# Transposes of dilated queries and keys spread through the running projection block, the keys' bank taken from another PSUM pool

## The chip, the cores and the metric

The kernel runs on one core of a Trainium2 chip. The metric is device time in microseconds for one launch: 1484.63 is the median of three runs of the kernel before (1481.72 to 1486.92).

## The reference

Two layers of a decoder trunk with 512 positions and a width of 1024, in float32. Each layer normalises its input, makes one wide projection from it, and feeds three mixers: a gated convolution (A), a causal latent attention with 8 heads (B), and a dilated sliding-window attention with three groups of 8 heads (C). The part that the change touches is C:

```python
dq = rmsnorm(dq.reshape(B, S, DIL_GROUPS, DIL_HEADS, DIL_HEAD_DIM), dil_q_norm_g[:, None, :])
dk = rmsnorm(dk.reshape(B, S, DIL_GROUPS, DIL_HEADS, DIL_HEAD_DIM), dil_k_norm_g[:, None, :])
for gi, (window, dilation) in enumerate(DIL_PATTERNS):
    o_g, lse_g = dilated_group_attention(dq[:, :, gi], dk[:, :, gi], dv[:, :, gi], slopes[gi],
                                         dilation, window // dilation)
alpha = jax.nn.softmax(jnp.stack(lses, axis=0), axis=0)
o_c = jnp.sum(alpha[..., None] * jnp.stack(outs, axis=0), axis=0)
```

The branches are gated, projected back, merged, projected once more and added to the input.

## The kernel before

Every large product is made of three matmuls in a reduced float32 format: operands are split into a high and a low part, and high x high, high x low and low x high are added up in one PSUM bank (`mm3`, lines 118 to 122). For weights the split runs on the chip: ScalarE casts the high part (line 114), VectorE subtracts it (line 115). Weight buffers rotate by five (`W_RAW`, `W_BUF`).

TensorE's order is written out by hand (`manual_schedule`, line 56): it runs its instructions in the order in which the program emits them. The order of VectorE, ScalarE and the DMA queue on SyncE is found by a scheduler that goes by priorities. Each engine works through its own list strictly in order.

The bulk of TensorE's work is a *filler*, a generator (lines 938 to 960) that yields after every *step*; a step is mostly one `mm3` of 512 columns, that is three matmuls (lines 120, 121, 122). The attention code asks the filler for some steps between its own pieces, so that attention and projections interleave. In the filler stand, one after the other: three convolution tiles, four gate tiles of B, nine *dilated blocks* (`dil_block`, each 32 steps in four PSUM banks of 8 steps, with 512 of the 4608 columns of queries, keys and values of C), a fourth convolution tile, four gate tiles of C, and the merge.

C is worked through in 12 *units* per layer: unit u belongs to the pair of heads p = u // 3 and to the group g = u % 3. Once a unit's queries and keys are projected and normalised, they are transposed (`dil_t`, lines 637 to 667): four 128x128 transposes (line 646) of the queries into one PSUM bank, four of the keys into another. The bank is then emptied. For g = 1 and 2 that is one ScalarE instruction (line 665). For g = 0 each half of the partitions is scaled by ScalarE (line 656), then a remainder is taken by VectorE (line 660); for keys ScalarE writes a second copy as well (line 658). The transposes of a block's units stand in the next block, after its first 15 steps (`T_LAG`); before, all banks of these units follow each other there, as one step each. Units 0, 3, 4, 7, 8 and 11 stand alone in their block, units 1 and 2, 5 and 6, 9 and 10 share one. After the last bank of a pair's third unit `ready` lets that pair's attention begin.

PSUM has eight banks, handed out by pools: `tr` two, `sc` two, `pj` two, `pv` one, `p1` one. `tr` is used by all transposes: those of dilated queries and keys, those of the probabilities of B (`mla_trans`, line 492) and of C (`dil_trans`, lines 779 and 788, emptied by VectorE in line 781 and ScalarE in line 790). `p1` is used by the preparation of B (`mla_p1`, and line 452 for its keys), which is over before the first dilated transposes, and once at the start of a layer (line 224).

The attention of a pair (`dil_main`) first makes its scores in four *rounds* (`dil_scores`): matmuls into the two `sc` banks (lines 691 and 695 for g = 0, in two rounds; line 701 for g = 1 and g = 2), then VectorE empties them with the bias added (line 709) and ScalarE takes the exponential (line 712). Six filler steps stand between rounds (`DIL_A`), and a round needs both `sc` banks empty again.

Of the kernel before, what the change touches and what calls it, by code (L numbers as in the profile page):

```python
# [27 lines left out]

F_LORA, F_P1, F_P2, F_MLA, F_TAIL, N_TAIL = 24, 6, 10, 1.2, 5.0, 28
NV_POOL, N_WAKE = 1, 11  # L30
LAG, PV_LAG, T_LAG = 2, 2, 15
P1_AT, P2_AT = (0, 8, 16), (6, 14, 22)
L_STEPS = ((5, 7, 8), (2, 4, 8))
DIL_A, DIL_GAP, DIL_B, DIL_C = 6, 29, 2, 2
# [11 lines left out]
def hybrid_kernel(ctx: ExitStack, tc: tile.TileContext, a: dict):  # L46
# [13 lines left out]
    def nm(s):  # L60
        uid[0] += 1
        return f"{s}_{uid[0]}"

    def psum(tag):
        return pp.tile([P, 512], F32, tag=tag, name=nm(tag), bufs=1 if tag in ("pv", "p1") else 2)
# [4 lines left out]
    def t2(shape, dt=F32):  # L70
        return sp.tile(shape, dt, tag="c2", name=nm("c2"), bufs=C2)
# [90 lines left out]
    def tok_nat(c):  # L162
        return slice(c * P, (c + 1) * P)

    def to_chunks(t, r):

        return t.rearrange("p (c x) -> p x c", c=NCH)[:, 32 * r:32 * r + 32]
# [43 lines left out]
    ps = psum("tr")  # L211
# [6 lines left out]
    for l in range(DEPTH):  # L218
# [347 lines left out]
        def dil_block(b):  # L566

            u0 = b // 3 * 4
            pieces = [(u0 + i // 3, i % 3) for i in range(b % 3 * 4, b % 3 * 4 + 4)]
            for u, s in pieces:  # L570
                m, p, g = dil_unit(u)
                if s == 2:
                    m["v"][g] = t2([P, NCH, P])
                    if g == 0:
                        m["bias"] = sp.tile([P, 2, S], F32, tag="bias", name=nm("bias"), bufs=1)
                        after_weights(nc.sync.dma_start(m["bias"], a["bias"][2 * p:2 * p + 2].rearrange("h p n -> p h n")))

            runs = []
            for i, (u, s) in enumerate(pieces):
                if runs and runs[-1][1] == u:  # L580
                    runs[-1][3] += 1
                else:
                    runs.append([i, u, s, 1])
            wq = []
            for q in range(4):
                dmas = []
                for i, u, s, n in runs:
                    c0 = u % 3 * 512 + u // 3 * P
                    if n == 1:
                        dmas.append((0, 1024, lambda t, i=i: t.rearrange("p (k n) -> p k n", k=2)[:, :, i * P:i * P + P],  # L590
                                     w_dil[:, 2 * q:2 * q + 2, s, c0:c0 + P]))
                        continue
                    for k in range(2):
                        o = k * 512 + i * P
                        dmas.append((o, o + n * P, lambda t, n=n: t.rearrange("p (s n) -> p s n", s=n),
                                     w_dil[:, 2 * q + k, s:s + n, c0:c0 + P]))
                wq.append(split_weights(1024, dmas))

            def evac(c, ps):
                for i, u, s, n in runs:  # L600
                    m, p, g = dil_unit(u)
                    nqk = min(n, 2 - s) if s < 2 else 0
                    if nqk:
                        nc.scalar.copy(m["nat"][g][:, c, s * P:(s + nqk) * P], ps[:, i * P:(i + nqk) * P])
                    if nqk < n:
                        nc.scalar.copy(m["v"][g][:, c], ps[:, (i + nqk) * P:(i + n) * P])

            yield from proj_n(wq, 512, evac)
            for u, s in pieces:
                if s == 2 and u % 3 == 0:  # L610

                    vt = dil[u // 3]["v"][0]
                    vscr = dp.tile([S, P], F32, tag="vscr", name=nm("vscr"))
                    nc.sync.dma_start(vscr.rearrange("(r p) d -> p r d", p=P), vt)
                    nc.sync.dma_start(vt, vscr.rearrange("(p c) d -> p c d", p=P))
                if s == 1:
                    dil_norm(u)
# [19 lines left out]
        def dil_t(p, g):  # L637
            m = dil[p]
            nat = m["nat"][g]
            m["qkt"].append([])  # L640
            for i in range(2):
                ps = psum("tr")
                for c in range(NCH):

                    dst = to_chunks(ps, c) if g == 0 else ps[:, tok_nat(c)]
                    nc.tensor.transpose(dst, nat[:, c, i * P:(i + 1) * P], ident)  # L646
                gg = prm2[:, 24 + g:25 + g] if i == 0 else prm[:, O_DK + g:O_DK + g + 1]
                if g == 0:

                    st = [t2([P, S], F32R) for _ in range(2)]  # L650
                    if i == 1:
                        lo = t2([P, S], F32R)
                    for h in range(2):
                        own = slice(64 * h, 64 * h + 64)
                        oth = slice(64 - 64 * h, 128 - 64 * h)
                        nc.scalar.activation(st[h][own], ps[own], AF.Copy, scale=gg[own])
                        if i == 1:
                            nc.scalar.activation(st[h][oth], ps[own], AF.Copy, scale=gg[own])
                        dst = lo[own] if i else st[h][oth]
                        nc.vector.scalar_tensor_tensor(out=dst, in0=ps[own], scalar=gg[own], in1=st[h][own],  # L660
                                                       op0=ALU.mult, op1=ALU.subtract)
                    m["qkt"][g] += [st, lo] if i else [st]
                else:
                    qt = t2([P, S])
                    nc.scalar.activation(qt, ps, AF.Copy, scale=gg)
                    m["qkt"][g].append(qt)
                yield
# [261 lines left out]
                    merged.append(hl)  # L929


        def transposes(units):
            for u in units:
                yield from dil_t(u // 3, u % 3)
                if u % 3 == 2:
                    ready[0] = u // 3

        def filler():
            for f in range(3):
                yield from conv_tile(f)  # L940
            for f in range(4):
                yield from z_tile(C_BZ, ob, "b", f)
            prev = []
            for b in range(9):
                gen = dil_block(b)
                for i in range(T_LAG if prev else 0):
                    next(gen)
                    yield
                yield from transposes(prev)
                yield from gen  # L950
                prev = [b // 3 * 4 + i for i in ((0,), (1, 2), (3,))[b % 3]]
            gen = conv_tile(3)
            for _ in range(T_LAG):
                next(gen)
                yield
            yield from transposes(prev)
            yield from gen
            for f in range(4):
                yield from z_tile(C_CZ, oc, "c", f)
            yield from gates()  # L960
# [32 lines left out]
        for dt in range(KD):  # L993
# [4 lines left out]
            ps = psum("pj")  # L998
# [99 lines left out]
```

## Time and profile before

| | |
|---|---|
| Median of three runs | 1484.63 us (1481.72 to 1486.92) |
| Profiled execution | 1483.1 us, span 1481.3 us |
| Mean granted clock of TensorE | 0.991 |
| TensorE (PE) matmul busy | 1434.1 us, 97% |
| VectorE (DVE) busy | 867.0 us, 59% |
| ScalarE (ACT) busy | 698.6 us, 47% |
| GpSimd (POOL) busy | 118.4 us, 8% |
| DMA queue 1, share of 16 engines | 32.8% |
| Chain that ended last | PE 81%, DVE 11%, ACT 5% |

TensorE has work nearly all the time, so time is won or lost where it waits; its waits are listed by the instruction that waited and the one that released it. A row of the timeline gives the start, the duration, the engine, the line, the output tile, the input tiles, the shapes and how many instructions were merged; in brackets stand the idle time before it and what ended it. `PEclk` in a table of windows is the granted clock as a share of its full speed of 2.4 GHz.

### The profile page before, as it was taken

How to read it: one execution, taken by the hardware profiler on the slowest of the kernel's cores; microseconds unless marked ns; L12 is line 12 of the kernel's file. 1: busy time of each engine (PE TensorE's matmuls, PEld its weight loads, DVE VectorE, ACT ScalarE, POOL GpSimd, SP SyncE). 2: the span in 40 equal slices, each digit the busy share in tenths (PEclk: the TensorE clock that was granted, in tenths of full speed). 3: DMA queues.
4: the chain of work that ended last, by engine and by line, in shares of the span. 5: the costliest groups of instructions: out<-in, count | busy, mean ns of one | idle time of the engine just before them, and what ended most of it. 6: DMA issues, size and time to landing. Idle time of an engine off the chain costs nothing.

```text
span 1481.3 us, 20395 instructions
## 1 busy us (share of the span) xinstructions
PE 1434.1 (97%) x7262; PEld 1181.6 (80%) x7262; DVE 867.0 (59%) x2295; ACT 698.6 (47%) x1600; POOL 118.4 (8%) x149
## 2 busy tenths in 40 slices
PE   9899999999979999999999999999999899999998
PEld 8778878877767878888898788788787677888887
DVE  8587775665566744343576867655664756534341
ACT  7455565656463432332354565656464553322220
POOL 0021221010010000000000212110100100000000
PEclk9999999999989999999999999999999999999999
DMA  8232222423223323333532321243252323333322
GB/s 248 75 100 58 61 72 58 128 74 87 78 73 106 89 79 92 100 115 97 171 113 73 99 67 37 73 119 81 58 134 82 81 63 88 86 99 100 114 71 85
DMA packets 237813, 136.52 MB, mean 92 GB/s; under 512 B 19856, under 2 KB 229392, under 8 KB 237712
## 3 DMA queue, kind: packets, MB, share of 16 engines
q1 hardware_dynamic: 237712, 135.23, 32.8%
q8 instruction: 57, 0.93, 0.3%
q14 instruction: 44, 0.36, 0.1%
HBM read 128.58 MB, written 6.62 MB: 91 GB/s over the span
## 4 chain that ended last, share of the span: by engine, by line
PE 81%; DVE 11%; ACT 5%; issue 2%; DMA 1%; SPq 0%; DVEq 0%; ACTq 0%
PE pj L120 20%; PE pj L121 19%; PE pj L122 19%; PE sc L122 4%; PE sc L121 3%; PE sc L120 3%; DVE wlo L115 2%; PE pv L810 2%; PE tr L646 1%; DMA wraw<-w_in 1%; ACT whi L114 1%; PE sc L701 1%; PE pv L509 1%; DVE c L175 1%; DVE s16a L628 1%
## 5 line engine op out<-in xcount | busy, mean ns | idle before, releaser
L115 DVE TENSOR_TENSOR wlo<-wraw,whi 128x1024 fp32r<-128x1024 f32 (+3 forms) x225 | 271.9, 1210 | 228.5 <-ACT whi L114 220.0
L114 ACT CAST whi<-wraw 128x1024 fp32r<-128x1024 f32 (+3 forms) x225 | 231.5, 1029 | 346.9 <-PE pj L121 189.0
L120 PE MATMUL pj<-hhi,whi 128*128 128x512 f32 x760 | 307.0, 404 | 2.9 <-ACT c L863 1.6
L121 PE MATMUL pj<-hlo,whi 128*128 128x512 f32 x760 | 298.6, 393 | 0.3 <-DVE hlo L284 0.3
L122 PE MATMUL pj<-hhi,wlo 128*128 128x512 f32 x760 | 298.6, 393 | 0.0
L120 PE MATMUL pj<-whi,hhi 128*128 128x512 f32 x576 | 238.8, 415 | 0.0
L121 PE MATMUL pj<-wlo,hhi 128*128 128x512 f32 x576 | 226.5, 393 | 0.0
L122 PE MATMUL pj<-whi,hlo 128*128 128x512 f32 x576 | 226.5, 393 | 0.0
L120 PEld LDWEIGHTS pj<-hhi,whi 128*128 128x128 f32 x760 | 143.8, 189 | 31.7 <-issue 2.1
L122 PEld LDWEIGHTS pj<-hhi,wlo 128*128 128x128 f32 x760 | 143.6, 189 | 30.9
L121 PEld LDWEIGHTS pj<-hlo,whi 128*128 128x128 f32 x760 | 144.0, 189 | 25.4 <-DVE hlo L284 0.9
L122 PEld LDWEIGHTS pj<-whi,hlo 128*128 128x128 f32 x576 | 108.8, 189 | 24.1
L120 PEld LDWEIGHTS pj<-whi,hhi 128*128 128x128 f32 x576 | 109.5, 190 | 22.7 <-issue 2.3
L121 PEld LDWEIGHTS pj<-wlo,hhi 128*128 128x128 f32 x576 | 109.4, 190 | 17.1
L712 ACT ACTIVATE c<-c,e 128x128 f32<-128x128 f32 (+1 forms) x192 | 80.1, 419 | 36.1 <-DVE e L709 36.0
L634 POOL TENSOR_TENSOR c<-c,s16c 128x512 f32<-128x512 f32 x48 | 51.0, 1084 | 371.7 <-DVE s16c L103 199.2
L709 DVE CUSTOM_DVE_ANT_0 c<-sc,bias 128x128 f32<-128x128 f32 (+1 forms) x192 | 53.0, 319 | 41.4 <-PE sc L695 41.3
L120 PE MATMUL sc<-c,whi 128*128 128x512 f32 x192 | 75.4, 393 | 0.0
L122 PE MATMUL sc<-c,wlo 128*128 128x512 f32 x192 | 74.8, 389 | 0.0
L121 PE MATMUL sc<-c,whi 128*128 128x512 f32 x192 | 74.7, 389 | 0.0
L479 ACT ACTIVATE c<-c,mst 128x128 f32<-128x128 f32 (+1 forms) x64 | 36.0, 562 | 68.0 <-DVE mst L477 67.7
L917 DVE SCALAR_TENSOR_TENSOR c<-c,sc 128x512 f32<-128x512 f32 x48 | 33.0, 687 | 37.2 <-PE sc L122 37.2
(202 smaller groups left out, 2149.9 us busy)
## 6 DMA issues: line engine op xcount, KB each, us to landing
wraw<-w_in SPq DMA_DIRECT2D x96, 512.0 KB, 3.7
wraw<-w_in SPq DMA_DIRECT2D x96, 192.0 KB, 3.4
wraw<-w_in SPq DMA_DIRECT2D x144, 128.0 KB, 2.7
wraw<-w_o SPq DMA_DIRECT2D x16, 512.0 KB, 3.9
bias<-bias SPq DMA_DIRECT2D x8, 512.0 KB, 3.8
wraw<-w_out_a SPq DMA_DIRECT2D x8, 512.0 KB, 3.3
wraw<-w_out_b SPq DMA_DIRECT2D x8, 512.0 KB, 3.4
wraw<-w_out_c SPq DMA_DIRECT2D x8, 512.0 KB, 3.3
```

The lines of the kernel that those rows point to most:

```text
L114: nc.scalar.copy(hi[:, c], raw[:, c])
L115: nc.vector.tensor_sub(lo[:, c], raw[:, c], hi[:, c])
L120: nc.tensor.matmul(out, lhs[0], rhs[0], start=start, stop=False)
L121: nc.tensor.matmul(out, lhs[0], rhs[1], start=False, stop=False)
L122: nc.tensor.matmul(out, lhs[1], rhs[0], start=False, stop=stop)
L175: nc.vector.tensor_sub(lo, src, hi)
L479: nc.scalar.activation(pr[:, :n_], pr[:, :n_], AF.Exp, bias=st[:, 0:1], scale=-1.0, accum_out=st[:, 2:3])
L634: eng.tensor_tensor(out=nv[:, i:i + 8], in0=nv[:, i:i + 8], in1=r2[:, i:i + 8].unsqueeze(2).to_broadcast([P, 8, 64]), op=ALU.mult)
L709: nc.vector.tensor_tensor_reduce(dst, src, b, op0=ALU.add, op1=ALU.min, scale=1.0, scalar=HIGHEST, accum_out=mc)
L712: nc.scalar.activation(dst, dst, AF.Exp, bias=mc, scale=-1.0, accum_out=sc_)
L810: nc.tensor.matmul(out, vs[g][:, c, hs[h]], rhs, start=(g == 0 and c == 0), stop=(g == 2 and c == 3), skip_group_check=True)
L917: nc.vector.scalar_tensor_tensor(out=ths[e], in0=ths[e], scalar=1.0, in1=ps, op0=ALU.add, op1=ALU.mult)
```

## The change

The banks of a unit's transposes no longer follow each other. `with_transposes` runs 15 steps of the block, then emits one bank, then four steps of the block (`T_GAP`), then the next bank, and so on. The query's bank stays in the pool `tr`; the key's bank comes from `p1`. A fourth convolution tile takes the place of a block for unit 11. Nothing is added or removed: both kernels have 192 transposes of line 646 and the same matmuls.

```diff
--- before.py
+++ after.py
@@ -28,7 +28,7 @@
 
 F_LORA, F_P1, F_P2, F_MLA, F_TAIL, N_TAIL = 24, 6, 10, 1.2, 5.0, 28
 NV_POOL, N_WAKE = 1, 11
-LAG, PV_LAG, T_LAG = 2, 2, 15
+LAG, PV_LAG, T_LAG, T_GAP = 2, 2, 15, 4
 P1_AT, P2_AT = (0, 8, 16), (6, 14, 22)
 L_STEPS = ((5, 7, 8), (2, 4, 8))
 DIL_A, DIL_GAP, DIL_B, DIL_C = 6, 29, 2, 2
@@ -639,7 +639,7 @@
             nat = m["nat"][g]
             m["qkt"].append([])
             for i in range(2):
-                ps = psum("tr")
+                ps = psum("p1" if i else "tr")
                 for c in range(NCH):
 
                     dst = to_chunks(ps, c) if g == 0 else ps[:, tok_nat(c)]
@@ -929,11 +929,20 @@
                     merged.append(hl)
 
 
-        def transposes(units):
+        def with_transposes(gen, units):
+
+            for _ in range(T_LAG if units else 0):
+                next(gen)
+                yield
             for u in units:
-                yield from dil_t(u // 3, u % 3)
+                for _ in dil_t(u // 3, u % 3):
+                    yield
+                    for _ in range(T_GAP):
+                        next(gen)
+                        yield
                 if u % 3 == 2:
                     ready[0] = u // 3
+            yield from gen
 
         def filler():
             for f in range(3):
@@ -942,19 +951,9 @@
                 yield from z_tile(C_BZ, ob, "b", f)
             prev = []
             for b in range(9):
-                gen = dil_block(b)
-                for i in range(T_LAG if prev else 0):
-                    next(gen)
-                    yield
-                yield from transposes(prev)
-                yield from gen
+                yield from with_transposes(dil_block(b), prev)
                 prev = [b // 3 * 4 + i for i in ((0,), (1, 2), (3,))[b % 3]]
-            gen = conv_tile(3)
-            for _ in range(T_LAG):
-                next(gen)
-                yield
-            yield from transposes(prev)
-            yield from gen
+            yield from with_transposes(conv_tile(3), prev)
             for f in range(4):
                 yield from z_tile(C_CZ, oc, "c", f)
             yield from gates()
```

What this does to the order, first on TensorE in the ninth block, where units 9 and 10 stand (`tr_` and `p_` are PSUM banks, `pj_` the block's accumulators, `c_` the projected queries and keys). Before:

```order
L122 MATMUL pj_4475<-whi_4415,hlo 128x512
L646 MATMUL tr_4525<-ident,c_783_3760 128x32x4 x4
L646 MATMUL tr_4564<-ident,c_783_3760 128x32x4 x4
L646 MATMUL tr_4578<-ident,c_830_4031 128x128 x4
L646 MATMUL tr_4585<-ident,c_830_4031 128x128 x4
L120 MATMUL pj_4475<-whi_4415,hhi 128x512
L121 MATMUL pj_4475<-wlo_4416,hhi 128x512
```

The four banks stand together, all in `tr`. With the change:

```order
L122 MATMUL pj_4475<-whi_4415,hlo 128x512
L646 MATMUL tr_4525<-ident,c_783_3760 128x32x4 x4
L120 MATMUL pj_4475<-whi_4415,hhi 128x512
L121 MATMUL pj_4475<-wlo_4416,hhi 128x512
L122 MATMUL pj_4475<-whi_4415,hlo 128x512
```

The block goes on behind the first bank. After three more steps, the same engine with the change:

```order
L122 MATMUL pj_4570<-whi_4399,hlo 128x512
L646 MATMUL p_930_4580<-ident,c_783_3760 128x32x4 x4
L120 MATMUL pj_4570<-whi_4399,hhi 128x512
L121 MATMUL pj_4570<-wlo_4400,hhi 128x512
L122 MATMUL pj_4570<-whi_4399,hlo 128x512
```

Four banks in a row became one bank, four steps, one bank in `p_930`, four steps, and so on.

VectorE where the second pair's scores meet the banks of unit 6 (`sc_` are score banks, `e_` their minima, `wlo_` low parts of weights). Before:

```order
L115 TENSOR_TENSOR wlo_3774<-wraw_3769,whi_3773 128x1024
L709 ISA c_771_3694,e_762_3648<-sc_3692,bias_2563 128x256
L709 ISA e_762_3648 128x1
L709 ISA c_772_3695,e_762_3648<-sc_3693,bias_2563 128x256
L709 ISA e_762_3648 128x1
L709 ISA c_771_3694,e_762_3648<-sc_3692,bias_2563 128x256
L709 ISA e_762_3648 128x1
L115 TENSOR_TENSOR wlo_3782<-wraw_3777,whi_3781 128x1024
L709 ISA c_772_3695,e_762_3648<-sc_3693,bias_2563 128x256
L709 ISA e_762_3648 128x1
L115 TENSOR_TENSOR wlo_3790<-wraw_3785,whi_3789 128x1024
```

The instructions of round two have only weights between them. With the change:

```order
L115 TENSOR_TENSOR wlo_3782<-wraw_3777,whi_3781 128x1024
L660 SCALAR_TENSOR_TENSOR c_768_3685<-p_765_3678,prm_106,c_766_3683 64x512
L709 ISA c_771_3697,e_758_3640<-sc_3695,bias_2563 128x256
L709 ISA e_758_3640 128x1
L115 TENSOR_TENSOR wlo_3790<-wraw_3785,whi_3789 128x1024
L660 SCALAR_TENSOR_TENSOR c_768_3685<-p_765_3678,prm_106,c_767_3684 64x512
L709 ISA c_772_3698,e_758_3640<-sc_3696,bias_2563 128x256
L709 ISA e_758_3640 128x1
L709 ISA c_771_3697,e_758_3640<-sc_3695,bias_2563 128x256
L709 ISA e_758_3640 128x1
L115 TENSOR_TENSOR wlo_4038<-wraw_4032,whi_4037 128x1024
L709 ISA c_772_3698,e_758_3640<-sc_3696,bias_2563 128x256
```

Two subtractions for the key's bank `p_765` now stand between the second round's score instructions (`sc_3695`, `sc_3696`), where before those of unit 6 were all ahead of the first round.

ScalarE at the same place. Before:

```order
L114 CAST whi_3773<-wraw_3769 128x1024
L114 CAST whi_3781<-wraw_3777 128x1024
L712 ACTIVATE c_771_3694,e_762_3648<-c_771_3694,e_762_3648 128x256
L114 CAST whi_3789<-wraw_3785 128x1024
L712 ACTIVATE c_772_3695,e_762_3648<-c_772_3695,e_762_3648 128x256
L114 CAST whi_4037<-wraw_4032 128x1024
L712 ACTIVATE c_771_3694,e_762_3648<-c_771_3694,e_762_3648 128x256
L712 ACTIVATE c_772_3695,e_762_3648<-c_772_3695,e_762_3648 128x256
```

Here too only weights stand between the exponentials. With the change:

```order
L114 CAST whi_3781<-wraw_3777 128x1024
L656 ACTIVATE c_766_3683<-p_765_3678,prm_106 64x512
L658 ACTIVATE c_766_3683<-p_765_3678,prm_106 64x512
L114 CAST whi_3789<-wraw_3785 128x1024
L656 ACTIVATE c_767_3684<-p_765_3678,prm_106 64x512
L658 ACTIVATE c_767_3684<-p_765_3678,prm_106 64x512
L114 CAST whi_4037<-wraw_4032 128x1024
L712 ACTIVATE c_771_3697,e_758_3640<-c_771_3697,e_758_3640 128x256
```

The four copies of the key's bank moved in between the casts of weights; before they stood ahead of the pair's first exponential.

## Rows read from the trace of the kernel before

**Rows 1.** Waits of TensorE: who waited, for whom, us in total, times, longest.
```profile
PE tr L646 <- ACT c L665: 9.2, 10, 2.8
PE tr L492 <- DVE c L660: 6.8, 4, 2.3
PE tr L646 <- DVE c L660: 6.0, 2, 3.3
...
PE sc L701 <- DVE e L709: 4.6, 4, 2.0
...
PE tr L646 <- DVE c L781: 1.1, 4, 0.3
```

**Rows 2.** Timeline of TensorE in the ninth block, layer 0.
```profile
422.69 1.03 PE L646 MATMUL tr<-ident,c 128*128 128x128 f32 x8
426.43 0.91 PE L646 MATMUL tr<-ident,c 128*128 128x128 f32 x4 [2.71 <-DVE c L660]
430.10 1.11 PE L646 MATMUL tr<-ident,c 128*128 128x128 f32 x4 [2.75 <-ACT c L665]
...
433.53 0.40 PE L120 MATMUL pj<-whi,hhi 128*128 128x512 f32 x1
```

**Rows 3.** Two windows: busy time by engine, PEclk, DMA share, GB/s.
```profile
240.00:250.00 10.00, 8.86 (x48) 7.26 (x47) 2.35 (x6) 4.17 (x10) 3.96 (x5) 1.00 0.00 0
...
422.00:435.00 13.00, 7.53 (x33) 5.95 (x32) 7.44 (x28) 7.43 (x17) 0.00 (x0) 0.74 0.16 43
```

**Rows 4.** Timeline of TensorE in the fifth block: two banks without a wait.
```profile
300.64 1.03 PE L646 MATMUL tr<-ident,c 128*128 128x128 f32 x8
301.43 0.48 PE L120 MATMUL pj<-whi,hhi 128*128 128x512 f32 x1
```

**Rows 5.** Timeline of TensorE in the second block, among the attention of B.
```profile
212.93 0.60 PE L646 MATMUL tr<-ident,c 128*128 128x128 f32 x4
215.81 0.30 PE L492 MATMUL tr<-ident,c 128*128 128x128 f32 x1 [2.28 <-DVE c L660]
```

**Rows 6.** Timeline of ScalarE, a query's bank of g = 0.
```profile
328.88 0.68 ACT L656 ACTIVATE c<-tr,prm 64x512 fp32r<-64x512 f32 x1 [0.33 <-PE tr L646]
330.37 1.39 ACT L656 ACTIVATE c<-tr,prm 64x512 fp32r<-64x512 f32 x2 [0.81 <-DVE c L660]
```

**Rows 7.** Timeline of VectorE, the same bank.
```profile
329.59 0.74 DVE L660 SCALAR_TENSOR_TENSOR c<-tr,prm,c 64x512 fp32r<-64x512 f32 x1 [2.35 <-ACT c L656]
```

**Rows 8.** Timeline of TensorE, rounds two and three of the second pair.
```profile
342.84 0.63 PE L691 MATMUL sc<-c,c 128*128 128x256 f32 x4
...
343.83 0.50 PE L120 MATMUL pj<-whi,hhi 128*128 128x512 f32 x1
...
348.12 1.16 PE L701 MATMUL sc<-c,c 64*128 64x128 f32 x16
349.21 0.50 PE L120 MATMUL pj<-whi,hhi 128*128 128x512 f32 x1
```

**Rows 9.** Timeline of VectorE, the last score instruction of round two.
```profile
347.06 0.42 DVE L709 CUSTOM_DVE_ANT_0 c<-sc,bias 128x256 f32<-128x256 f32 x1
```

**Rows 10.** Timeline of ScalarE there: a copy of projections and a cast of weights.
```profile
341.14 0.38 ACT L604 COPY c<-pj 128x256 f32<-128x256 f32 x1
...
344.83 1.05 ACT L114 CAST whi<-wraw 128x1024 fp32r<-128x1024 f32 x1 [1.42 <-PE pj L122]
```

**Rows 11.** The page's costliest groups: busy us, mean ns of one, idle before.
```profile
L115 DVE TENSOR_TENSOR wlo<-wraw,whi 128x1024 fp32r<-128x1024 f32 (+3 forms) x225 | 271.9, 1210 | 228.5 <-ACT whi L114 220.0
...
L712 ACT ACTIVATE c<-c,e 128x128 f32<-128x128 f32 (+1 forms) x192 | 80.1, 419 | 36.1 <-DVE e L709 36.0
```

**Rows 12.** Timeline of TensorE, a wait before round four of the third pair.
```profile
416.16 2.45 PE L701 MATMUL sc<-c,c 64*128 64x128 f32 x16 [2.04 <-DVE e L709]
418.54 0.79 PE L120 MATMUL pj<-whi,hhi 128*128 128x512 f32 x1
...
419.92 0.39 PE L120 MATMUL pj<-whi,hhi 128*128 128x512 f32 x1
```

## The prediction

> **What bounds the kernel now.** I read the waits of TensorE first, since by the table it is busy for 97% of the span and a gain must come out of its waits. Three of the rows in [rows 1] belong to the banks that the change moves: the transposes wait 9.2 us for the emptying of such a bank by ScalarE, 6.0 us for VectorE's part of it and 1.1 us for other banks of the pool `tr`; the transposes of B's probabilities, which use the same two banks, wait 6.8 us. Together that is 23.1 us over both layers. No row there names a DMA, so I leave transfers out. Next I read the timeline around the longest of these waits. In the ninth block the third and fourth bank stand still for 2.71 and 2.75 us until one of the two `tr` banks is empty [rows 2]. The reader is to see one thing more there: after the second wait the matmuls are slow. The windows say why: the granted clock is 0.74 of the full speed between 422 and 435 us, that is, part of this stretch ran at 1.2 GHz, while it is 1.00 between 240 and 250 us, where there are only short waits [rows 3].
>
> **What the change removes.** Two banks without any wait take 0.79 us, from the first transpose to the matmul behind them [rows 4]. In the ninth block four banks and the six matmuls of two steps take 433.53 - 422.69 = 10.84 us [rows 2]. Without waits they would take 2 x 0.79 + 1.4 = 3.0 us (a step of three matmuls takes 0.7 us: the six steps between rounds two and three take 348.12 - 343.83 = 4.29 us [rows 8]). So this place costs 7.9 us in a layer, of which 5.5 us are listed as waits; 2.4 us are the slow clock. I count the second layer, with the same order, as the same: 4.8 us that the list of waits doesn't show. The 16 other waits in the list cost a little more than is listed: the bank of 212.93 would have been done after 0.79 / 2 = 0.39 us, but the next transpose starts after 2.88 us [rows 5], so 2.5 us are lost where 2.28 are listed, 0.2 us more each, 3.2 us for 16. The price of the order as it was is then 23.1 + 4.8 + 3.2 = 31.1 us.
>
> With the change each bank is followed by four steps, 2.8 us, and every second one goes to `p1`, so a bank of `tr` and one of `p1` come round only every 6 to 7 us. A bank of g = 1 or 2 is emptied by one ScalarE instruction. A query's bank of g = 0 takes four instructions in a strict chain: ScalarE starts at 328.88, VectorE at 329.59, ScalarE's second half waits 0.81 us for VectorE and starts at 330.37 [rows 6, 7], about 3 us in all; a key's bank, with two copies more, 4.4 us. Both fit into the new distance. The changed order also shows that the attention's positions hardly move: `ready` comes later, but the pairs' scores start at most a few steps later, since the pairs don't wait for it. So I take all 31.1 us as gone at these places. Spreading makes some 30 more places where transposes interrupt the matmuls (48 banks stand alone instead of 18 groups). A single bank shows a duration of 0.60 us, half of two in a row is 0.52 [rows 4, 5], so it may cost up to 0.08 us each, 2.4 us in all; I take nothing, since that tail lies beside the next matmul. The lists of SyncE and GpSimd hold the same instructions, with a few DMAs exchanged against neighbours.
>
> One residue stays. Query banks still share `tr` with the transposes of C's probabilities, at two places in a layer with only one step between. The row for this has four waits with 0.3 us as the longest [rows 1]. I take 0.5 us at each of four places, 2.0 us; the bounds are 0 and the 2.2 us of four waits of twice 0.28 us.
>
> **What the change adds.** The emptying now falls between other work, and VectorE and ScalarE run strictly in order. The order of the second pair is the place to fear: before, unit 6 was emptied before its first round of scores; now the four ScalarE copies of its key stand between casts of weights, and the two VectorE subtractions between the instructions that empty the score banks of round two. I follow it from the start of unit 6's query bank as 0. TensorE: bank 0.4, round one 1.0, four steps 2.85, key bank 0.4, one step 0.8, so round two starts at 5.4, and it ends 1.0 later (343.83 - 342.84 [rows 8]); with six steps of 4.3 us round three is due at 10.7. ScalarE: query copies and three exponentials (0.42 each [rows 11]) until 4.1, a copy and the first cast (0.38 and 1.05 [rows 10]) to 5.3, the fourth exponential and two copies to 6.2, the second cast to 7.2, two key copies of 0.7 to 8.6, the third cast to 9.6, two key copies to 11.0, the fourth cast to 12.0. VectorE can subtract the key's first half only then: 8.65 to 9.4; a score instruction of 0.35, a weight's low part of 1.2 [rows 11], the second half after ScalarE's copies from 11.05 to 11.8, two score instructions, the fourth low part, and the last score instruction at 14.0. So round three, due at 10.7, waits until 14.1: 3.4 us. Before, that last instruction ended at 347.48, and round three came at 348.12 without a wait [rows 8, 9]. A wait of such length has cost the clock: after the 2.04 us at 416.16 the round took 2.38 us to the next matmul where it takes 1.09, and the next step 1.38 where it takes 0.8 [rows 8, 12], 1.9 us in all. I take 3.4 + 1.9 = 5.3 us, 10.6 us for both layers. The bounds are 0 (casts early enough that the chain keeps pace) and 21.2 us (the fourth round, or the first pair's third, is late by as much again).
>
> The first pair meets unit 3's banks in the same way, but its key's chain ends before round two, and I count no wait. For the third pair the end of the block moves one step closer to round two, so VectorE gets that block's normalisation done up to 0.7 us sooner against the rounds: the 2.04 us wait [rows 12] shrinks, 1.4 us for both layers, between 0 and 7.8 us (the whole wait with its clock).
>
> In ScalarE's chain there is a point on which the Trainium skill could be read otherwise: its page PSUM — Partial Sum Buffer (section Terms) says that different 32-partition quadrants of one bank may be accessed by two engines at the same time. The second half of a query's bank lies in other quadrants than the half that VectorE reads, so by the rule the wait of 0.81 us needn't be there, the chain would be some 0.7 us shorter and the total 1.4 us lower. The trace shows the wait, and the sum goes by it.
>
> **The sum.** -31.1 + 2.0 + 10.6 - 1.4 = -19.9 us against the profiled execution's 1483.1 us, which gives 1463.2; the median of the runs lies 1.5 us higher. I forecast 1463.5.
>
> **The rivals.** *The new wait doesn't come* (0.17): the casts get ahead of the key's copies because TensorE's releases come earlier than I think. For it: in the trace the second cast waited 1.42 us for TensorE [rows 10], which is the slack that moves. Against it: the order is fixed and puts the copies in front of the third cast. Then -30.5 us: 1453.
>
> *More is given back* (0.14): round four of the second pair, or round three of the first, is late as well, by another 5.3 us per layer. For it: all three engines' slack there is below 1 us [rows 8, 9]. Against it: a wait of TensorE lets the others catch up. 1474.
>
> *No difference* (0.08): `p1` has one bank where the two banks of `tr` could overlap, so waits for a key's bank of 4.4 us replace those for `tr`. It needs the queues of ScalarE and VectorE to be some 3 us behind at nearly every unit, while these engines are busy for 47% and 59% of the span. About 1482.
>
> *Slower* (0.05): the emptying of g = 0 units collides with the rounds not at one place but at all of them, two rounds in each of three pairs, 12 waits of 5.3 us, 64 us. It decides from the sixth wait on (the gain without any of them is 30.5 us, and 30.5 / 5.3 = 5.8). For it: such units are emptied in six instructions over two in-order engines, and every round of g = 0 and 1 has casts among it. Against it: the first and third pair's order has the subtractions ahead of round two or behind round four. 1483 + 64 - 31 = 1516.
>
> *The clock falls at every bank* (0.01). Four dozen short interruptions, each with the 1.9 us of a slow resumption, would cost 91 us less 31: 1543. The windows speak against it: 1.00 with waits in it [rows 3]. The Trainium skill's TensorE: Matmul & The Clock Gate (section A second HAM failure mode: psum-queue depth-cycling) describes such a loss from cycling through banks; by that rule the change would be slower, and the trace agrees with it only behind some of the long waits.
>
> The rest (0.55) is my forecast, 1455 to 1470 by itself. The range of 1450 to 1477 adds the two neighbours. What a measurement can tell from no change is 0.3%, 4.5 us: faster 0.86, the same 0.08, slower 0.06.
>
> **What would show it.** In the profile after, the waits of lines 646 and 492 for lines 660 and 665 should be below 3 us together, the ninth block without slow matmuls and with a granted clock near 1. The wait of line 701 for line 709 should have grown from 4.6 to about 10 us, with a new entry before round three of the second pair in either layer. I am wrong if the waits for lines 660 and 665 remain, if a line of matmuls waits for weights, or if the score waits grow by more than 20 us.

## The result

The changed kernel takes 1461.7 us (median of four runs, 1459.37 to 1462.64), the kernel before in the same comparison 1483.18 us (1479.2 to 1486.92). The ratio is 0.9853 with a 95% interval of 0.9823 to 0.9883: faster by 1.5%. Measured once more, again beside the kernel before, it was 1459.47 against 1481.78 us, a ratio of 0.9855 (0.9835 to 0.9874). The forecast was 1463.5. The profiled execution takes 1462.64 us with a span of 1460.8 us, 20.5 us less than before.

The first line of the page after that counts is the busy time by engine.

```profile
span 1460.8 us, 20392 instructions
PE 1434.1 (98%) x7262; PEld 1183.1 (81%) x7262; DVE 862.0 (59%) x2295; ACT 699.0 (48%) x1600; POOL 117.2 (8%) x149
```

TensorE's busy time is 1434.1 us, to the tenth what it was before. Span minus busy time is its idle time: 1481.3 - 1434.1 = 47.2 us before, 26.7 us after. So the gain between these two executions is idle time. Busy time contains what matmuls lose at the slow clock, and the equal sums hide two changes in it, which the windows below show. The list of TensorE's waits says which idle time went (who waited, for whom, us in total, times, longest):

```profile
PE sc L701 <- DVE e L709: 8.4, 6, 1.9
...
PE tr L492 <- DVE c L175: 0.4, 2, 0.2
```

The waits of lines 646 and 492 for lines 660, 665 and 781 [rows 1] are no longer there; the wait of line 701 for line 709 has grown from 4.6 to 8.4 us. In the ninth block, TensorE's timeline after has in place of [rows 2]:

```profile
420.28 0.60 PE L646 MATMUL tr<-ident,c 128*128 128x128 f32 x4
420.63 0.48 PE L120 MATMUL pj<-whi,hhi 128*128 128x512 f32 x1
...
423.47 0.60 PE L646 MATMUL p<-ident,c 128*128 128x128 f32 x4
...
426.68 0.60 PE L646 MATMUL tr<-ident,c 128*128 128x128 f32 x4
...
429.89 0.60 PE L646 MATMUL p<-ident,c 128*128 128x128 f32 x4
```

Four banks 3.2 us apart, none with a bracket for idle time, and the next matmul 0.35 us behind the first transpose. At the place of [rows 5], the next transposes of B's probabilities start with no wait either:

```profile
211.79 0.62 PE L646 MATMUL tr<-ident,c 128*128 128x128 f32 x4
...
213.49 0.27 PE L492 MATMUL tr<-ident,c 128*128 128x128 f32 x1
```

The new wait stands before round three of the second pair, where before [rows 8] there was none. The first row is the bank of unit 6's queries, from which the prediction counts:

```profile
331.28 0.60 PE L646 MATMUL tr<-ident,c 128*128 128x128 f32 x4
...
341.70 0.39 PE L122 MATMUL pj<-whi,hlo 128*128 128x512 f32 x1
343.99 0.49 PE L701 MATMUL sc<-c,c 64*128 64x128 f32 x2 [1.90 <-DVE e L709]
345.47 2.07 PE L701 MATMUL sc<-c,c 64*128 64x128 f32 x14 [0.99 <-DVE e L709]
347.47 0.79 PE L120 MATMUL pj<-whi,hhi 128*128 128x512 f32 x1
...
350.62 0.63 PE L121 MATMUL pj<-wlo,hhi 128*128 128x512 f32 x1
...
351.74 0.40 PE L121 MATMUL pj<-wlo,hhi 128*128 128x512 f32 x1
...
414.37 1.54 PE L701 MATMUL sc<-c,c 64*128 64x128 f32 x16 [1.36 <-DVE e L709]
```

The round waits for one bank, then for the other, 2.89 us together; the rest of it takes 2.07 us, and a matmul 0.63 us instead of 0.40, until 351.5: the slow clock. The last line is the third pair's fourth round [rows 12], whose wait fell from 2.04 to 1.36 us. VectorE at the new wait shows why the last score instruction is late [rows 9]:

```profile
339.90 0.74 DVE L660 SCALAR_TENSOR_TENSOR c<-p,prm,c 64x512 fp32r<-64x512 f32 x1
340.57 0.41 DVE L709 CUSTOM_DVE_ANT_0 c<-sc,bias 128x256 f32<-128x256 f32 x1
...
340.98 1.23 DVE L115 TENSOR_TENSOR wlo<-wraw,whi 128x1024 fp32r<-128x1024 f32 x1
342.39 0.76 DVE L660 SCALAR_TENSOR_TENSOR c<-p,prm,c 64x512 fp32r<-64x512 f32 x1 [0.18 <-ACT c L658]
343.16 0.42 DVE L709 CUSTOM_DVE_ANT_0 c<-sc,bias 128x256 f32<-128x256 f32 x1
...
344.99 0.42 DVE L709 CUSTOM_DVE_ANT_0 c<-sc,bias 128x256 f32<-128x256 f32 x1
```

Round two's matmuls were over at 337.7. Its last score instruction comes at 344.99, behind both subtractions for unit 6's key, the second of which had to wait for ScalarE's copies, and behind two low parts of weights (line 115, the second among the rows left out). The order was fixed by the program, and what stood behind the waiting subtraction ran after it. The Trainium skill has the rule in TensorE: Matmul & The Clock Gate (section Architectural detail: the array is 16× 32×32, not 1× 128×128): ScalarE and VectorE are strictly first in, first out. The trace agrees, with the 0.18 us of that wait and the order of the rows.

Windows of both kernels show where the slow clock stood (start and end, length, busy time by engine, then PEclk, DMA share, GB/s). Before:

```profile
410.00:420.00 10.00, 7.96 (x38) 6.34 (x38) 9.79 (x53) 6.20 (x26) 2.81 (x3) 0.83 0.37 107
420.00:440.00 20.00, 14.53 (x64) 11.70 (x63) 11.34 (x51) 10.26 (x31) 1.27 (x2) 0.83 0.11 29
...
1140.00:1156.00 16.00, 11.72 (x75) 9.20 (x73) 11.95 (x62) 11.46 (x44) 4.09 (x4) 1.00 0.47 127
...
1150.00:1170.00 20.00, 14.04 (x62) 11.33 (x61) 12.83 (x62) 10.72 (x32) 2.05 (x2) 0.83 0.12 30
```

After:

```profile
340.00:360.00 20.00, 17.10 (x84) 13.43 (x83) 11.41 (x58) 14.17 (x52) 2.04 (x2) 0.83 0.57 152
410.00:440.00 30.00, 28.64 (x137) 23.21 (x136) 24.17 (x109) 20.46 (x60) 4.09 (x4) 0.94 0.39 105
1060.00:1080.00 20.00, 17.10 (x88) 13.35 (x87) 12.73 (x59) 15.66 (x55) 2.04 (x2) 0.91 0.59 156
1130.00:1150.00 20.00, 18.71 (x91) 14.99 (x90) 14.16 (x77) 13.86 (x51) 4.09 (x4) 0.91 0.23 69
```

A window's length times (1 - PEclk) is the time that the clock took, if TensorE was busy throughout; at 1.2 instead of 2.4 GHz the slow stretch itself is twice as long. Slow time inside a wait costs nothing.

Before, 10 x 0.17 = 1.7 us were lost at the third pair's fourth round in the first layer, and none in the second (the third row). In the ninth block of either layer 20 x 0.17 = 3.4 us mean a slow stretch of 6.8 us, of which the last wait [rows 2] takes 2.75 us, so the matmuls lost (6.8 - 2.75) / 2 = 2.0 us. That makes 1.7 + 2 x 2.0 = some 5.8 us. After, the slow stretch at the new wait in the first layer is 6.8 us long as well; it ends at 351.5, so it began some 0.8 us before the wait was over, and 3.0 us were lost. The new wait in the second layer and the third pair in both add 1.8 us each: 8.4 us. (Two digits of PEclk leave some tenths open.)

So the ninth block is free of slow clock, but the new wait and the third pair have more of it: some 2.5 us more in all. As the busy time is the same, the rest of TensorE's work must have become shorter by about as much.

### The profile page after: what moved, and what is told of

Same layout as the page of the kernel before. It is cut to its first block, busy times and chain, and to the rows that moved or that the text cites. A ratio compares the mean times of both kernels' runs of the same rounds, so it can differ in the third digit from the quotient of the medians.

```text
span 1460.8 us, 20392 instructions
## 1 busy us (share of the span) xinstructions
PE 1434.1 (98%) x7262; PEld 1183.1 (81%) x7262; DVE 862.0 (59%) x2295; ACT 699.0 (48%) x1600; POOL 117.2 (8%) x149
## 4 chain that ended last, share of the span: by engine, by line
PE 86%; DVE 9%; ACT 2%; issue 2%; DMA 1%; SPq 0%; DVEq 0%; ACTq 0%
PE pj L120 21%; PE pj L121 21%; PE pj L122 21%; PE sc L122 4%; PE sc L121 4%; PE sc L120 4%; DVE wlo L115 2%; PE pv L810 2%; PE sc L701 1%; PE pv L509 1%; PE tr L492 1%; PE tr L779 1%; PE tr L646 1%; DVE c L875 1%; PE p L122 1%
## 5 line engine op out<-in xcount | busy, mean ns | idle before, releaser
L120 PE MATMUL pj<-whi,hhi 128*128 128x512 f32 x576 | 242.8, 422 | 0.0
L435 POOL TENSOR_TENSOR c<-c,c 128x256 fp32r<-128x256 f32 x16 | 18.3, 1148 | 445.5 <-PE p L122 433.7
```

The costliest lines, as they stand in the source:

```text
L120: nc.tensor.matmul(out, lhs[0], rhs[0], start=start, stop=False)
L435: nc.gpsimd.tensor_sub(vt[:, :, :, 64:128], v_, vt[:, :, :, 0:64])
```

## The experiments

All times are medians, and the ratio to the kernel before has its 95% interval. The kernel before was measured again each time: 1481.12 us beside e1 to e4, 1481.78 beside e5 to e8, 1479.31 beside e9 to e11. So across these groups the ratios compare better than the times. Idle is span minus TensorE's busy time in the one profiled execution, which need not be the median run.

| run | us | ratio to before | idle us | busy us |
|---|---|---|---|---|
| before | 1483.18 | 1 | 47.2 | 1434.1 |
| after | 1461.7 | 0.9853 (0.9823 to 0.9883) | 26.7 | 1434.1 |
| e1 ready late | 1459.26 | 0.9858 (0.9841 to 0.9874) | 29.7 | 1425.0 |
| e2 ten steps | 1455.95 | 0.9830 (0.9814 to 0.9847) | 26.9 | 1428.0 |
| e3 spread only | 1467.67 | 0.9901 (0.9882 to 0.9920) | 30.5 | 1429.4 |
| e4 other pool only | 1468.47 | 0.9914 (0.9900 to 0.9928) | 37.5 | 1429.7 |
| e5 after again | 1459.47 | 0.9855 (0.9835 to 0.9874) | 26.9 | 1431.3 |
| e6 shift and back | 1447.82 | 0.9775 (0.9761 to 0.9790) | 22.1 | 1424.2 |
| e7 two shifts | 1453.55 | 0.9815 (0.9800 to 0.9830) | 25.6 | 1425.9 |
| e8 gap of two | 1461.78 | 0.9871 (0.9857 to 0.9886) | 33.1 | 1428.2 |
| e9 shift inside | 1448.87 | 0.9789 (0.9771 to 0.9806) | 21.1 | 1424.9 |
| e10 one step | 1450.32 | 0.9797 (0.9780 to 0.9814) | 21.9 | 1425.9 |
| e11 e6 with `tr` | 1454.30 | 0.9828 (0.9809 to 0.9847) | 25.9 | 1426.3 |

**The two halves of the change: e3 and e4.** In e3 the banks are spread, but keys stay in `tr`:

```diff
-                ps = psum("p1" if i else "tr")
+                ps = psum("tr")
```

> Banks spread by four steps as in the changed kernel, the keys' bank back in tr. Theory one (distance alone carries the gain: a tr bank comes round every 6.5 us, emptying takes 3 to 4.4 us): within 3 us of 1461.7, no wait of line 646 for 660 or 665 above 0.5 us. Theory two (the other pool is needed because B's probability transposes turn tr over faster): waits of line 492 for 660 return, 6.8 us in all as before, 1467 to 1470 us.

The new entry in the list of TensorE's waits in its trace:

```profile
PE tr L646 <- DVE c L781: 4.6, 2, 2.3
```

B's waits did not return, against theory two, and there is no wait for lines 660 or 665, so distance alone removes those. But the median is not theory one's either: one wait of 2.30 us in each layer appeared, for line 781. That is not all of the 6.0 us above 1461.7. The six runs of e3 lie between 1461.76 and 1470.17 us, and the profiled one is the fastest; its granted clock is 0.995, that of the three slowest 0.988 to 0.990. Where those lost more to the clock no trace shows. The new wait's place in TensorE's timeline of e3:

```profile
445.38 0.66 PE L646 MATMUL tr<-ident,c 128*128 128x128 f32 x4 [2.30 <-DVE c L781]
```

And VectorE's timeline there:

```profile
442.67 2.18 DVE L875 SCALAR_TENSOR_TENSOR c<-c,prm,c 128x384 f32<-128x384 f32 x8
444.77 0.55 DVE L781 COPY c<-tr 128x384 f32<-128x384 f32 x1
```

A bank of unit 11 waits for the other user of `tr`, the third pair's probabilities, whose copy stands behind eight additions of the convolution tile. That is what `p1` is for. In e4 the order of before is kept and only the pool of the keys changes (the same line of the diff, the other way round, in the kernel before).

> The order of before, all banks of a block's units in a row, but the keys' bank from p1. Theory (distance carries most): in the ninth block the second key still waits for the first key's emptying, some 5 us with the slow clock behind it; only B's waits (line 492 for 660, 6.8 us, and part of line 646 for 665) go; no new wait before round three: 1471 to 1477 us. Rival (the pool carries most): 1461 to 1466 us, or below, since the new wait of the spread order isn't paid.

Of the waits of [rows 1] on the moved banks, the list of e4 keeps one entry above 0.9 us:

```profile
PE p L646 <- DVE c L660: 12.9, 2, 6.5
```

The waits are the theory's: those of lines 492 and 646 of [rows 1] went, but for a few tenths and the one key bank in the ninth block, where 5.5 us of waits in a layer [rows 2] became one wait of 6.5 us. The time, 1468.47, lies between the theory's range and the rival's, so the pool alone removes more than I gave it. Each half alone gives 0.9 to 1.0%, both 1.5%.

**The new wait: e1 and e2.** e1 lets a pair begin only after all units of its block:

```diff
                         next(gen)
                         yield
+            for u in units:
                 if u % 3 == 2:
                     ready[0] = u // 3
```

> A pair's scores may start only after the last bank of all units of its block, so unit 6 is emptied before round one of the second pair; everything else is as in the changed kernel. Theory (the new wait before round three comes from unit 6's key bank being emptied among round two's score instructions): the wait of line 701 for line 709 falls from 8.4 to below 4 us, the granted clock between rounds two and four is back at 1.00, and the time falls by 10.6 us by the terms of the prediction, or by about 14 us by what the timeline shows (2.9 us of wait and some 4 us of slow matmuls per layer): 1448 to 1451 us. Rival (that wait is what the pair pays anyway: too many casts beside the rounds): the same wait stands before round three at its new place, the time stays within 3 us of 1461.7.

The new entries in e1's list of TensorE's waits:

```profile
PE tr L788 <- DVE c L781: 4.5, 2, 2.9
PE tr L646 <- POOL c L634: 3.7, 4, 1.3
PE pj L120 <- ACT c L606: 3.4, 2, 1.7
```

The theory of the cause holds: line 701's wait is gone altogether, and there is no slow stretch at the second pair's rounds (PEclk 1.00 from 340 to 360). The time, 1459.26, is the rival's, though not for the rival's reason: three new kinds of wait, 11.6 us together, stand in the list. The second pair starts later, what follows it moved too, and met other work. e2 moves the third round alone:

```diff
-            for _ in dil_scores(p):
-                yield DIL_A
+            for r, _ in enumerate(dil_scores(p)):
+                yield DIL_A + (4 if p == 1 and r == 1 else 0)
```

> Ten filler steps instead of six between rounds two and three of the second pair; the emptying of unit 6 stays between them. Theory (round three comes 3 us too early): four steps more are 2.8 us, about the 2.9 us of the wait, so most of it goes and the clock stays up: 10 to 14 us less, 1448 to 1452 us. Rival one (the queue is bound by TensorE's releases of weights, so VectorE's last score instruction moves later with every step added): the wait stays, the time within 3 us of 1461.7. Rival two (only the listed wait goes, the slow clock has another cause): 5 to 6 us less, 1456.

The new entry in e2's list that decides:

```profile
PE tr L779 <- DVE c L781: 5.0, 2, 2.5
```

Before round three 0.27 us is left of 2.89, so rival one (the wait moves along) is out. But all that follows stands four steps later, and 5.0 us are paid where the third pair's probabilities are transposed. At 1456 it looks like rival two; it is not, for the clock came back with the wait (PEclk 1.00 from 340 to 360, in the second layer from 1060 to 1080).

**The gain without the move: e5 and e6.** e5 is the changed kernel again, as the measure for e6 to e8.

> The changed kernel once more, so that the other runs of this call have it beside them. From its ratio of 0.9853 and 1481 us for the kernel before: 1458 to 1462 us. If the clock falls between 40 and 56 us of the span in its profiled execution, the span is some 3 us longer than in one without.

It came as expected, 1459.47. In a stretch that no edit touches the two traces of this kernel differ: between 40 and 100 us of the span PEclk is 0.97 in this one and 0.91 in the first, 60 x 0.06 = 3.6 us for it, but between 0 and 40 us it is 0.96 here and 1.00 there, 1.6 us against it. Some 2 us are left of the 2.6 us between the two spans. The profile of the kernel before has 0.91 and 1.00 there, as the changed kernel's first one, so those two compare well. On top of the edit of e2, e6 takes the four steps back from the long gap before the second pair's probabilities:

```diff
             dil_weights(p)
-            yield DIL_GAP
+            yield DIL_GAP - (4 if p == 1 else 0)
```

> As the run with ten steps between rounds two and three of the second pair, but the long gap before that pair's probability transposes is four steps shorter, so all that follows stands where the changed kernel has it. Theory (the last two runs lost their gain because the pairs behind moved, into the normalisation of unit 10 and into VectorE's copies): no wait of lines 779 or 788 for line 781 and none of line 646 for line 634 above 0.6 us, the wait of line 701 for 709 at about 3 us (the third pair's fourth round, 1.36 and 1.29 us, stays), the clock near round three of the second pair at 1.00: idle time of TensorE 5 us and slow clock 5 us less than in the changed kernel, 1449 to 1452 us. Rival (TensorE's gain is taken back by whatever comes next, as any gain in this stretch): within 3 us of the run with ten steps, 1456.

What is left of line 701's waits, as TensorE's timeline of e6 shows it at round three of the second pair and round four of the third:

```profile
343.97 1.16 PE L701 MATMUL sc<-c,c 64*128 64x128 f32 x14 [0.27 <-DVE e L709]
...
407.29 1.54 PE L701 MATMUL sc<-c,c 64*128 64x128 f32 x16 [1.36 <-DVE e L709]
```

And the windows around them:

```profile
340.00:360.00 20.00, 19.73 (x111) 15.79 (x110) 11.75 (x66) 15.22 (x59) 2.05 (x2) 1.00 0.55 144
400.00:440.00 40.00, 38.64 (x209) 31.59 (x208) 33.07 (x129) 26.04 (x69) 6.15 (x6) 1.00 0.44 120
```

1447.82 us, 11.7 us less than e5: the theory, and a little more (it had 1449 to 1452). The idle time falls by 4.8 us against e5, the busy time by 7.1. The clock is 1.00 at the second pair; it is also 1.00 at the third, where the same 1.36 us are waited as in the changed kernel, and this second part is a gain that the theory didn't have. No version that was run has a lower median; the intervals of e9 and e10 overlap with this one's.

**A second repair that fails: e7, e9, e10.** The third pair's fourth round still waits. e7 gives it three steps and takes three from that pair's gap; e10 does so with one; e9 moves that pair's round three two steps earlier instead. The edit of e7 against e6:

```diff
+            more = {(1, 1): 4, (2, 2): 3}
             for r, _ in enumerate(dil_scores(p)):
-                yield DIL_A + (4 if (p, r) == (1, 1) else 0)
+                yield DIL_A + more.get((p, r), 0)
             dil_weights(p)
-            yield DIL_GAP - (4 if p == 1 else 0)
+            yield DIL_GAP - (0, 4, 3, 0)[p]
```

> The same, and also three steps more before round four of the third pair, three less in that pair's long gap. Theory (that wait too is VectorE coming late by some 1.3 us, beside the block's normalisation, and the slow clock of 1.7 us per layer behind it hangs on the wait): the wait of line 701 for 709 below 1 us in all, 2.7 us less idle time and up to 3.4 us less slow clock than the run before it: 1444 to 1448 us. Rival (VectorE's list is late throughout and the round waits the same after three steps more, or the probability transposes now wait): no gain, 1449 to 1452 us.

The new entries in e7's list of TensorE's waits:

```profile
PE tr L788 <- DVE c L781: 4.4, 2, 2.2
PE p L646 <- DVE c L660: 1.7, 2, 1.0
```

The fourth round no longer waits (0.5 us are left of line 701's 3.2), but 6.1 us are paid for it: 1453.55 us, slower than e6 and above the rival's range too. e10 has `(2, 2): 1` and a gap of `(0, 4, 1, 0)`:

> The version with the second pair repaired, and the third pair's fourth round one step later with one step less in its long gap (the run before it had three). Theory (the 2.2 us that the probability transposes waited in the run with three steps grow with the steps taken from the gap, 0.7 us each): the fourth round's wait falls by 0.7 us to 0.6 us, the waits of line 788 for 781 stay below 0.8 us each: 1446 to 1448 us. Rival (any move of the third pair's scores reorders VectorE so that its copies of probabilities come late): waits of line 788 above 2 us again, 1451 to 1454 us.

TensorE's timeline of e10 at the fourth round and at the probability transposes:

```profile
407.66 1.54 PE L701 MATMUL sc<-c,c 64*128 64x128 f32 x16 [0.68 <-DVE e L709]
...
436.40 0.66 PE L788 MATMUL tr<-ident,c 128*128 128x128 f32 x4 [1.06 <-DVE c L781]
```

0.7 us won, 1.06 us paid, in each layer, and 1450.32 us lie between the theory's range and the rival's. I read it so, though no run tests it: that pair's group weights can only be formed after round four, and VectorE then comes late with the probabilities. The edit of e9 against e6:

```diff
-                yield DIL_A + (4 if (p, r) == (1, 1) else 0)
+                yield DIL_A + {(1, 1): 4, (2, 1): -2, (2, 2): 2}.get((p, r), 0)
```

> The version with the second pair's third round four steps later (four steps less in its long gap), and the third pair's third round two steps earlier with its fourth at its old place. Theory (the fourth round waits 1.36 and 1.29 us because round three's score instructions come late on VectorE; two steps are 1.4 us; what follows doesn't move, so nothing is paid back): the wait of line 701 for 709 falls from 3.2 to below 1 us, no wait of line 788 for 781: 1444 to 1446 us. Rival (VectorE is held by the block's normalisation, which doesn't move, so score instructions land behind it all the same, or round three itself now waits for round two): the same wait of 1.3 us or more, 1447 to 1450 us.

TensorE's timeline of e9 at the fourth round:

```profile
405.56 1.54 PE L701 MATMUL sc<-c,c 64*128 64x128 f32 x16 [1.36 <-DVE e L709]
```

The wait is the same to a hundredth, as the rival had it. Round three's matmuls come 8.2 instead of 6.8 us ahead of round four, but on VectorE its score instructions still stand behind the block's normalisation (VectorE's timeline of e9; the last row is the first of eight):

```profile
402.19 0.68 DVE L628 TENSOR_REDUCE s16a<-c 128x8 f32<-128x512 f32 x1
...
402.87 0.29 DVE L709 CUSTOM_DVE_ANT_0 c<-sc,bias 128x128 f32<-128x128 f32 x1
```

**One size, and the pool once more: e8 and e11.** e8 has `T_GAP = 2`.

> Two steps instead of four between banks. Theory (distance against emptying time): a pair of banks comes round every 3.6 us while a key's bank of g = 0 takes 4.4 us to empty, so the ninth block's second key waits about 1 us in each layer and B's probability transposes wait again for some tenths; unit 6's key bank is emptied two steps earlier against round two, so the wait before round three falls from 2.9 to about 1.5 us: the sum is within 3 us of the changed kernel. Rival one (four steps were needed): waits of lines 646 and 492 for lines 660 and 665 of 8 us and more, 1466 to 1472 us. Rival two (the wait before round three doesn't depend on the key's place): it stays at 2.9 us.

The list of TensorE's waits in e8, the rows that changed:

```profile
PE tr L788 <- DVE c L781: 5.4, 2, 2.7
PE sc L701 <- DVE e L709: 4.9, 4, 2.1
PE p L646 <- DVE c L660: 4.0, 2, 2.3
```

The place of the key decides about the wait before round three: with two steps its bank comes before round one, and nothing is left of the wait there (the theory had 1.5 us). The waits of line 701 that are listed stand before fourth rounds: the third pair's is back at 2.1 us. The ninth block's key waits twice what I expected, and the first pair's probabilities wait 2.7 us, which no theory had. The sum is the changed kernel's (0.9871 to 0.9855). e11 is e6 with the keys in `tr`:

> The version with the second pair repaired, the keys' bank back in tr. Theory one (the other pool is worth what the trace of the spread-only run shows, the wait of unit 11's bank for the third pair's probabilities, 2.3 us in each layer, 4.6 us in all, and a slow clock of up to 3.4 us behind it): 1452 to 1456 us, B's waits (line 492 for 660) still nothing. Theory two (that wait only came from the spread-only run's own timing): within 2 us of 1447.8.

The new entry in the list of TensorE's waits in e11:

```profile
PE tr L646 <- DVE c L781: 4.6, 2, 2.3
```

1454.3 against 1447.8, theory one: the wait of e3 came back unchanged, 2.30 us in each layer. So the other pool is worth 6.5 us here (by the ratios 0.5%, some 8 us), and all of the listed wait is at unit 11.

## Why the prediction was right

*What is removed* was right in its places. The 23.1 us of listed waits went. For the ninth block 4.8 us of slow clock were counted; its slow stretch is gone in both layers, and by the windows it had cost 2 x 2.0 us. The 3.2 us for "0.2 us more" at 16 waits are not in the idle time, which fell by what the lists account for (23.1 us, 0.6 of line 788, 0.9 of waits for weights, less 3.8 that line 701 gained and 0.4 of small ones, 20.4 of the 20.5 us). They can stand in the busy time, whose part without slow clock fell by some 2.5 us. That is one execution against one, so the size of this term stays open.

*The residue* was mis-sized. I took 2.0 us for queries that share `tr` with C's probabilities. No such wait is left, and the 0.6 us of line 788 went as well. e3 shows what would have been there: the conflict is with a key, not a query, and costs 2.3 us a layer. I had not seen that the copy of the probabilities may stand behind the convolution tile.

*What is added* was right in mechanism and nearly in size. Counted from unit 6's query bank at 331.28, the two subtractions start at 8.62 and 11.11 us (forecast 8.65 and 11.05), and the second bank of round three comes at 14.19 (forecast 14.1). The waits before it are 1.90 + 0.99 us (forecast 3.4): two of the round's matmuls, 0.49 us, fit in between. The slow clock behind them cost 3.0 us in one layer and 1.8 in the other (forecast 1.9 each): 5.8 + 4.8 = 10.6 us, as forecast, but the agreement to the tenth is luck: the wait was taken too long and the slow clock too short. e1, e2 and e6 show that it is this mechanism: with the key emptied earlier, or the round later, wait and slow clock both go.

*The third pair* was half right. The waits shrank by 2.04 - 1.36 us in the first layer, and from 1.96 to 1.29 in the second, as forecast (1.4 us in all). But in the second layer the clock, which had stayed up, now fell behind it, 1.8 us, so this place lost some 0.4 us, outside the bounds of 0 to 7.8 us of gain. The step "the whole wait with its clock" assumed that a shorter wait can only cost less clock; the rows show that it doesn't follow.

*The sum*: forecast -19.9, measured -20.5 us between profiled executions. As idle time I had -18.9 and as slow clock -1.0; measured are -20.5 us of idle time, some +2.5 of slow clock and some -2.5 of other busy time. The missing residue (2.6 us with line 788's waits) and waits that I hadn't counted (0.9 us for weights, 0.6 before the second pair's fourth round) outweigh the third pair's clock and the smaller price of the ninth block. That the total agrees to 0.6 us is in part luck. The last step of the sum also has a slip: 1463.2 with the 1.5 us by which the median lies higher is 1464.7, not 1463.5; the median came out at 1461.7.

*The rivals.* "The new wait doesn't come" is refuted by its 2.89 us in either layer. "More is given back" was not seen: round four of the second pair and round three of the first follow without a wait. "No difference" needed waits for a key's bank in `p1`, and none is listed; "slower" needed waits at many rounds, and there are new ones at one round in each layer. "The clock falls at every bank" is refuted: 48 banks stand alone, and four of them in the ninth block pass at a PEclk of 1.00 (420 to 440 us). The Trainium skill's section A second HAM failure mode: psum-queue depth-cycling (in TensorE: Matmul & The Clock Gate) tells of a loss from cycling through banks; here no single bank shows it, and the slow stretches among C's scores stand behind waits of lines 701 for 709.

## What to carry to other kernels

Work for in-order engines is not free because it is short: ask behind which instruction each piece will stand, and whether a matmul waits for the one behind it. Spreading users of a scarce buffer took most of their waits away; another pool then helped at the one place where two users still met. When a local repair of a wait gives little, look whether it moved what follows: the same four steps were worth 3.5 us when everything behind them moved (e2), and 11.7 us when they were taken back from a gap with slack (e6). And equal busy times of an engine don't mean that nothing changed in them: a slower clock in one place can hide a gain in another.

## What was not expected of the hardware

The clock's fall is not set by the length of the last wait alone. After 1.36 us before the third pair's fourth round it fell in the changed kernel (PEclk 0.94 from 410 to 440) and did not in e6 (1.00 from 400 to 440); before the change 1.96 us in the second layer left it up (1.00 from 1140 to 1156). In e11 the wait of 2.30 us for line 781 stands in both layers, and the clock fell at it in the first (0.91 from 440 to 460) and not in the second (1.00 from 1160 to 1180). What else decides stays open.

And executions of one program differ by what the clock does near their start: PEclk 0.97 against 0.91 between 40 and 100 us, 0.96 against 1.00 before that, some 2 us in all. The scatter between runs of one kernel is of that size in e5 (1458.36 to 1461.51 us) and larger in e3 (1461.76 to 1470.17), where the slower runs have the lower granted clock.
